# A hybrid encoder layer on one core: the products in the order v, k, q, the last gate's halves between them three, one, two, and the first weights on ScalarE's queue

## The chip, the cores and the metric

The kernel runs on one core of a Trainium2 chip. Its time is the device time of one execution in microseconds (us); less is better. The core's engines are named as the profile names them: PE (TensorE's matmuls; PEld its weight loads), DVE (VectorE), ACT (ScalarE), POOL (GpSimd) and SP (SyncE, which issues most of the DMAs). Each engine takes its instructions in the order in which the program lists them and waits, where it must, at the head of its own queue.

## The reference, cut to what matters

One layer on 512 tokens of width 1024. The normalised input is projected to 8192 columns: a pooling branch, an LRU branch, q, k and v of an attention with eight heads of 128, and three gates of 1024 columns each.

```python
h = rms_norm(x, norm_mix[l])
proj = jnp.einsum('bsd,dc->bsc', h, w_in[l])
u_pool, u_lru, q, k, v, g_logits = jnp.split(proj, splits, axis=-1)
gates = jax.nn.sigmoid(g_logits + b_gate[l]).reshape(B, S, N_BRANCH, D_MODEL)
...
qh = rms_norm(q.reshape(B, S, SB_HEADS, SB_HEAD_DIM), q_norm[l])
kh = rms_norm(k.reshape(B, S, SB_HEADS, SB_HEAD_DIM), k_norm[l])
vh = v.reshape(B, S, SB_HEADS, SB_HEAD_DIM)
y_sb = stick_breaking_attention(qh, kh, vh).reshape(B, S, SB_WIDTH)
merged = (gates[:, :, 0] * jnp.einsum('bsc,cd->bsd', y_pool, w_branch[l, 0])
          + gates[:, :, 1] * jnp.einsum('bsc,cd->bsd', y_lru, w_branch[l, 1])
          + gates[:, :, 2] * jnp.einsum('bsc,cd->bsd', y_sb, w_branch[l, 2]))
x = x + jnp.einsum('bsd,de->bse', merged, w_out[l])
```

A SwiGLU network with its own norm and residual follows. q and k are normed per head, v is not. The three products do not depend on each other; the attention needs all three.

## The kernel before

**Arithmetic.** Every weight is float32 and is used as a high and a low part: ACT copies the raw weights to `whi` (line 101), DVE subtracts that from the raw weights into `wlo` (line 102), and PE makes three matmuls of a pair (high by high, high by low, low by high). `raw`, `whi` and `wlo` have three buffers each, so the weights of a half can be made ready when the half three places ahead of it has been used.

**Stages.** (1) The head: token tiles `xt` and the first weights `raw0` are loaded, split (`hu`, `hi0`, `lo0`), and PE runs eight matmuls on a constant tile (`WARM`, line 349) until they are there; then come the gates of the first branch. (2) The LRU projections in four chunks with the second branch's gates between them; the LRU's own work (convolution, gates, scans) runs beside PE on ACT and DVE and reaches into stage 3. (3) q, k and v, described below. (4) The pooling branch, with the attention's work for eight heads spread over it and over the branch products of stage 5. (6) The output projection, (7) the network.

**The products q, k and v.** Each 1024 by 1024 product is done with seven block products instead of eight, named in `ORDER` (line 131): "11", "12", "S2", "S1", "S3", "S4", "22"; the S ones use sums of weight blocks, which DVE makes (`qkv_sum`, line 145). A block product has two halves of twelve matmuls (`tok_product`, lines 703 to 715, matmuls on line 712), each with its own pair `whi`, `wlo`. PE accumulates in PSUM; ACT copies a first part out (`snap`, line 722), DVE adds the rest (`final`, line 726). That leaves four blocks r of a product, (0,0), (1,1), (0,1) and (1,0), in this order. `post` (line 678) then norms q and k: ACT squares the block, DVE sums the squares (line 683) and scales the sum (line 684), POOL raises it to the power -1/2 (`rsqq`, line 256), and DVE refines this in four small instructions (lines 257 to 260). For q the result, `qrs`, goes with its negative (line 700) into the scale of a later sigmoid, so the block itself is stored as it is; for k, `krs`, ACT multiplies the block in eight instructions (line 698) before it is stored. The stores go out on POOL's queue into `qd`, from which the attention loads its heads (`at`, line 889).

**The third branch's gates.** Four chunks of 256 columns, each in two halves of 24 matmuls (`half_chunk`). The last chunk runs in stage 4; the six halves of the others stand between the block products, at the places in `AFTER` (line 172): after "12", "S3" and "22" of q and of k. The third product, v, has none.

**What sets the order.** The program is recorded in the order of the code; small tasks stand in lists (`bg`, `abg`) from which `tick` takes one after each piece of PE work. A scheduler then orders each engine's instructions by priorities, which `tc.high_priority` raises for weight splits. The order is fixed when the kernel is built.

Of the kernel before, what the change touches and what calls it, by code (L numbers as in the profile page):

```python
# [25 lines left out]
QSCALE = float(HD) ** -0.5  # L26
NEG = -1.0e30
EARLY = 300
WARM = 8
GBUFS = 27  # L30
NDIRECT = 2
KD = 4
# [31 lines left out]
def layer_kernel(ctx: ExitStack, tc: tile.TileContext, x, xt, vecs, w_in, w_pool, w_rg, w_ig,  # L64
                 w_branch, w_out, w_fg, w_fu, w_fd, out):
    nc = tc.nc
# [14 lines left out]
    def b4(shape, name, tag="b", dt=F32):  # L81
        bufs = {"w": NAW, "t": NAT, "b": NAB}[tag]
        return pools["ap0"].tile([P] + shape, dt, tag=tag, name=name, bufs=bufs)
# [5 lines left out]
    def cols(ap, k0, nk, c0, nc_):  # L89
        return ap[k0 * P:(k0 + nk) * P, c0:c0 + nc_].rearrange("(k p) c -> p k c", p=P)  # L90
# [25 lines left out]
    def add_gate(br, c):  # L116
        add_chunk256(("gate", br, c), w_in, 5120 + br * 1024 + c * 256)
# [14 lines left out]
    WITH = {"11": "11", "12": "21", "S2": "T2", "S1": "T1", "S3": "T3", "S4": "22", "22": "T4"}  # L132
    CH = {"11": 0, "12": 0, "21": 1, "22": 1}
    KH = {"11": 0, "12": 1, "21": 0, "22": 1}
    qraw = {}

    def qkv_raw(t, nm, i):
        if (t, nm, i) not in qraw:
            qraw[t, nm, i] = r = b4([2, 512], f"qw{t}{nm}{i}", "w")
            nc.sync.dma_start(r, cols(w_in, 4 * KH[nm] + 2 * i, 2, 2048 + t * 1024 + CH[nm] * 512, 512))  # L140
        return qraw[t, nm, i]
# [27 lines left out]


    AFTER = {}
    for n, (t, nm) in enumerate(((0, "12"), (0, "S3"), (0, "22"), (1, "12"), (1, "S3"), (1, "22"))):
        AFTER[t, nm] = divmod(n, 2)

    for n in range(4):
        add_direct(("first", n), cols(w_in, 2 * n, 2, 5120, 512), 2, 512)
# [2 lines left out]
    for n in (0, 1, 2, 4, 3, 5, 6, 7):  # L179
        if n < 4:  # L180
            add_lru(n)
        else:
            add_gate(1, n - 4)
    for t in range(3):
        for nm in ORDER:
            add_seven(t, nm, 0)
            add_seven(t, nm, 1)
            if (t, nm) in AFTER:
                c, half = AFTER[t, nm]
                add_direct(("gate", 2, c, half), cols(w_in, 4 * half, 4, 7168 + c * 256, 256), 4, 256)  # L190
# [41 lines left out]
    vt = cst.tile([P, NV], F32, tag="vt", name="vt")  # L232
# [102 lines left out]
    with ExitStack() as first:  # L335
# [11 lines left out]
        wps = pb.tile([P, 2, S], F32, tag="mm", name="warm_ps")  # L347
        for i in range(WARM):
            nc.tensor.matmul(wps[:, 0, :], warm[:, 0:P], warm, start=True, stop=True)
# [21 lines left out]
        raw0 = wp.tile([P, 2, 512], F32, tag="raw", name="raw0")  # L371
        ready["first", 0] = hi0, lo0
        src0 = cols(w_in, 0, 2, 5120, 512)
        nc.scalar.dma_start(vt, vecs)
        for k in range(2):
            load_xt(k)
            nc.sync.dma_start(raw0[:, k, :], src0[:, k, :])
            dve.tensor_copy(hi0[:, k, :], raw0[:, k, :])
            dve.tensor_tensor(lo0[:, k, :], raw0[:, k, :], hi0[:, k, :].bitcast(F32), ALU.subtract)
            make_h(k)  # L380
# [293 lines left out]
        def store(t, i, j, r):  # L674
            nc.gpsimd.dma_start(rows(t, i, j), r)


        def post(t, i, j, r):
            if t < 2:
                sq = b4([2, 512], f"sq{t}{i}{j}")  # L680
                s_ = cst.tile([P, 8], F32, tag="ssq", name=f"ssq{t}{i}{j}", bufs=2)
                act(sq, r, AF.Square)
                dve.tensor_reduce(s_, sq.rearrange("p a (b d) -> p (a b) d", d=HD), AX.X, ALU.add)
                dve.tensor_scalar(s_, s_, 1.0 / HD, EPS, ALU.mult, ALU.add)
                bg.append(lambda: post2(t, i, j, r, s_))
            else:
                store(t, i, j, r)

        def post2(t, i, j, r, s_):

            y = cst.tile([P, 8], F32, tag="krs", name=f"krs{i}{j}", bufs=2) if t else \
                qrs[:, 0, 2 * j:2 * j + 2, 4 * i:4 * i + 4]
            y3 = y.rearrange("p (a b) -> p a b", a=2) if t else y
            rsqrt(y3, s_.rearrange("p (a b) -> p a b", a=2), (2, 4), f"q{t}{i}{j}")
            if t:
                v = r.rearrange("p a (b d) -> p (a b) d", d=HD)
                for n in range(8):
                    act(v[:, n, :], v[:, n, :], AF.Copy, scale=y[:, n:n + 1])
            else:
                dve.tensor_scalar(qrs[:, 1, 2 * j:2 * j + 2, 4 * i:4 * i + 4], y3, -1.0, None, ALU.mult)  # L700
            store(t, i, j, r)

        def tok_product(t, nm, ps, first):
            bh, bl = BQ[WITH[nm]]
# [10 lines left out]
                    tick()  # L715

        gate2 = {}
        for t in range(3):
            ps = {}
            r = {}  # L720

            def snap(key, src):
                r[key] = b4([2, 512], f"r{t}{key[0]}{key[1]}")
                act(r[key], src, AF.Copy)

            def final(key, src):
                dve.tensor_tensor(r[key], r[key], src, ALU.add)
                bg.append(lambda t=t, key=key, v=r[key]: post(t, *key, v))

            def bank(nm):  # L730
                ps[nm] = pb.tile([P, 2, 512], F32, tag="mm", name=f"ps_q{t}{nm}")
                return ps[nm]

            for nm in ORDER:
                if nm in ("11", "12", "S1", "22"):
                    bank(nm)
                dst = {"S2": "11", "S3": "11", "S4": "S1"}.get(nm, nm)
                tok_product(t, nm, ps[dst], dst == nm)
                if nm == "11":
                    snap((0, 0), ps["11"])  # L740
                elif nm == "12":
                    final((0, 0), ps["12"])
                elif nm == "S2":
                    snap((0, 1), ps["11"])
                elif nm == "S1":
                    snap((1, 1), ps["S1"])
                elif nm == "S3":
                    final((1, 1), ps["11"])
                    snap((1, 0), ps["11"])
                elif nm == "S4":  # L750
                    final((0, 1), ps["S1"])
                else:
                    final((1, 0), ps["22"])
                if (t, nm) == (0, "S3"):
                    for f, c in ((lru_input, 3), (lru_scan, 2), (lru_scan, 3), (lru_store, 2), (lru_store, 3)):
                        step(of(f, c))
                if (t, nm) in AFTER:
                    c, half = AFTER[t, nm]
                    if half == 0:
                        gate2[c] = chunk_psum(("gate", 2, c), pb)  # L760
                    half_chunk(gate2[c], ("gate", 2, c), half, hn, 1)
                    if half == 1:
                        gate_store(2, c, gate2[c], True)
# [258 lines left out]
    with ExitStack() as ffn:  # L1022
# [21 lines left out]
        for c in range(4):  # L1044
# [5 lines left out]
            for j in range(2):  # L1050
                k = 2 * c + j
                if c % 2 == 0:
                    x1p[c // 2, j] = mp.tile([P, 2, S], F32, tag="m", name=f"x1{c}{j}")
                t = x1p[c // 2, j][:, c % 2, :]
# [77 lines left out]
        CH = {"11": 0, "12": 0, "21": 1, "22": 1}  # L1132
        KH = {"11": 0, "12": 1, "21": 0, "22": 1}

# [6 lines left out]
        def load_a(c):  # L1141
            for nm in ("11", "21", "22", "12"):
                raw[c, nm] = t = corner([2, 4, P], f"w{c}_{nm}")
                for w in range(2):
                    if c < DOWN:
                        ap, c0 = (w_fg, w_fu)[w], c * 256
                    else:
                        ap, c0 = w_fd, (c - DOWN) * 512 + w * 256
                    nc.sync.dma_start(t[:, w], cols(ap, KH[nm] * 4, 4, c0 + CH[nm] * P, P))

# [100 lines left out]
        for m in range(4):  # L1251
            t = fp.tile([P, 2, S], F32, tag="mm", name=f"ps_d{m}")
# [38 lines left out]
        for kc in range(KD, last + 1):  # L1291
            split_act(kc + 1)
            ah, al = split.pop(kc)
            for e in range(2):
# [3 lines left out]
                for j in range(4):  # L1298
# [5 lines left out]
                    if kc == last:  # L1304
                        t = x1[m]
# [64 lines left out]
```

## Time and profile before

| what | value |
|---|---|
| median of 3 runs | 939.15 us (937.56 to 939.16) |
| the profiled execution | 938.85 us, span 937.0 us |
| mean granted TensorE clock over the span | 0.998 |
| PE, DVE, ACT, POOL busy, share of the span | 99%, 76%, 52%, 5% |
| DMA | 124.13 MB, mean 132 GB/s |
| first product q, k, v (us from the span's start) | about 144 to 300 |

The span is the time from the first to the last instruction of the profiled execution; its own time is 1.85 us more. In a row of the timeline the first number is the start, the second the time busy, then engine, line, operation, output and inputs; in square brackets stands how long the engine had been idle and what ended that. A row of waits has the total, the number of waits and the longest. The starts of matmuls are the thing to read: their ends overlap.

### The profile page before, as it was taken

Reading aid. Unit: us, or ns where it says so; the run is one execution under the profiler, and the core shown is the slowest. Engines: PE = TensorE matmul, PEld = TensorE weight load, DVE = VectorE, ACT = ScalarE, POOL = GpSimd, SP = SyncE. Lnnn points to the kernel's source line nnn. Section 1 sums busy time; section 2 is a strip of 40 time slices with the busy share of each in tenths; the row PEclk is TensorE's granted clock in tenths of the full one; section 3 lists DMA queues with packets and bytes.
Section 4 is the critical chain, followed back from the end, with each engine's and each line's share of the span. In section 5 each row is a group of like instructions: output and inputs, shape, how many; then the busy total and the mean of one; then the engine's idle time right before and its main releaser. Section 6 shows DMA issues by size and latency. Waiting matters only on the chain.

```text
span 937.0 us, 13039 instructions
## 1 busy us (share of the span) xinstructions
PE 925.5 (99%) x5090; PEld 796.5 (85%) x5090; DVE 709.8 (76%) x890; ACT 489.6 (52%) x660; POOL 45.2 (5%) x69
## 2 busy tenths in 40 slices
PE   9999999899999999999999999999999999999998
PEld 6888778787878888788888888889999999988898
DVE  6797889777696699866865545699888888787465
ACT  6545997545655465644643234454554555653232
POOL 2000000222121000000000000000000000000000
PEclk9999999999999999999999999999999999999999
DMA  9484351652714934155532344355533334523001
GB/s 333 124 286 135 113 180 68 211 171 68 247 58 145 281 117 130 61 166 173 153 91 90 98 136 149 91 143 141 144 91 97 106 105 138 165 97 105 1 29 63
DMA packets 126894, 124.13 MB, mean 132 GB/s; under 512 B 7408, under 2 KB 105712, under 8 KB 126832
## 3 DMA queue, kind: packets, MB, share of 16 engines
q1 hardware_dynamic: 122800, 109.07, 38.2%
q0 software_dynamic: 3888, 14.16, 4.4%
q8 instruction: 40, 0.66, 0.3%
q14 instruction: 22, 0.18, 0.1%
q10 hardware_dynamic: 144, 0.06, 0.0%
HBM read 107.02 MB, written 16.25 MB: 132 GB/s over the span
## 4 chain that ended last, share of the span: by engine, by line
PE 82%; DVE 8%; ACT 5%; issue 3%; POOL 2%; DMA 0%; POOLq 0%; DVEq 0%; ACTq 0%
PE ps_y L1182 11%; PE ps_x L1182 8%; PE ps_br L227 5%; PE ps_br L229 5%; PE ps_br L228 5%; PE ps_q L712 3%; PE ps_d L227 3%; PE ps_d L228 3%; PE ps_d L229 3%; PE ps_gate L625 3%; PE ps_dy L1182 2%; DVE wlo L102 2%; PE ps_gate L227 2%; PE ps_gate L228 2%; PE ps_gate L229 2%
## 5 line engine op out<-in xcount | busy, mean ns | idle before, releaser
L101 ACT ACTIVATE whi<-raw 128x1024 fp32r<-128x1024 f32 x93 | 98.4, 1058 | 149.1 <-PE ps_br L228 46.2
L102 DVE TENSOR_TENSOR wlo<-raw,whi 128x1024 fp32r<-128x1024 f32 x93 | 113.5, 1221 | 63.8 <-ACT whi L101 58.6
L1172 ACT ACTIVATE wh_S<-w_S 128x1024 fp32r<-128x1024 f32 x44 | 46.6, 1061 | 56.6 <-PE ps_y L1182 25.6
L1173 DVE TENSOR_TENSOR wl_S<-w_S,wh_S 128x1024 fp32r<-128x1024 f32 x44 | 53.6, 1221 | 12.8 <-ACT wh_S L1172 12.6
L1172 ACT ACTIVATE wh<-w 128x1024 fp32r<-128x1024 f32 x33 | 35.0, 1062 | 49.0 <-issue 12.9
L102 DVE TENSOR_TENSOR wlo<-qw,whi 128x1024 fp32r<-128x1024 f32 x36 | 43.9, 1220 | 17.3 <-ACT whi L101 17.2
L1173 DVE TENSOR_TENSOR wl<-w,wh 128x1024 fp32r<-128x1024 f32 x33 | 40.3, 1222 | 17.4 <-ACT wh L1172 17.4
L101 ACT ACTIVATE whi<-qw 128x1024 fp32r<-128x1024 f32 x36 | 37.9, 1055 | 26.1 <-PE ps_q L712 17.6
L227 PE MATMUL ps_gate<-HH,whi 128*128 128x512 f32 x128 | 50.1, 392 | 0.0
L229 PE MATMUL ps_gate<-HH,wlo 128*128 128x512 f32 x128 | 49.9, 390 | 0.0
L228 PE MATMUL ps_gate<-HL,whi 128*128 128x512 f32 x128 | 49.8, 389 | 0.0
L227 PE MATMUL ps_d<-ah,whi 128*128 128x512 f32 x112 | 43.7, 391 | 0.0
L228 PE MATMUL ps_d<-al,whi 128*128 128x512 f32 x112 | 43.6, 389 | 0.0
L229 PE MATMUL ps_d<-ah,wlo 128*128 128x512 f32 x112 | 43.6, 389 | 0.0
L1160 DVE TENSOR_TENSOR w_S<-w,w 128x1024 f32<-128x1024 f32 x22 | 26.9, 1223 | 3.4 <-PE ps_d L228 2.9
L229 PEld LDWEIGHTS ps_gate<-HH,wlo 128*128 128x128 f32 x128 | 24.0, 188 | 5.3 <-DVE wlo L102 0.4
L227 PEld LDWEIGHTS ps_gate<-HH,whi 128*128 128x128 f32 x128 | 24.0, 188 | 5.2 <-issue 0.4
L228 PEld LDWEIGHTS ps_gate<-HL,whi 128*128 128x128 f32 x128 | 24.0, 188 | 4.9
L1160 DVE TENSOR_TENSOR w_S<-w,w_S 128x1024 f32<-128x1024 f32 x22 | 26.9, 1223 | 0.6
L933 DVE TENSOR_TENSOR_SCAN E<-K,zero 128x511 f32<-128x511 f32 (+3 forms) x32 | 25.5, 812 | 1.1 <-ACT K L928 1.1
L227 PE MATMUL ps_br<-yph,whi 128*128 128x512 f32 x64 | 25.6, 400 | 0.0
L227 PE MATMUL ps_pool<-HH,whi 128*128 128x512 f32 x64 | 25.6, 400 | 0.0
(634 smaller groups left out, 3015.7 us busy)
## 6 DMA issues: line engine op xcount, KB each, us to landing
raw<-in_w_in_dram SPq DMA_DIRECT2D x39, 512.0 KB, 4.9
qw<-in_w_in_dram SPq DMA_DIRECT2D x24, 512.0 KB, 4.7
raw<-in_w_branch_dram SPq DMA_DIRECT2D x24, 512.0 KB, 3.5
w<-in_w_ffn_gate_dram SPq DMA_DIRECT2D x36, 256.0 KB, 3.8
w<-in_w_ffn_up_dram SPq DMA_DIRECT2D x36, 256.0 KB, 4.2
raw<-in_w_ffn_down_dram SPq DMA_DIRECT2D x14, 512.0 KB, 3.5
qd<-r POOLq DMA_DIRECT2D x12, 512.0 KB, 3.4
at<-qd SPq DMA_DIRECT2D x24, 256.0 KB, 5.5
```

What stands on the lines that cost most here:

```text
L101: act(hi, raw, AF.Copy)
L102: dve.tensor_tensor(lo, raw, hi.bitcast(F32), ALU.subtract)
L227: nc.tensor.matmul(ps, lh, rh, start=start, stop=False, skip_group_check=skip)
L228: nc.tensor.matmul(ps, lh, rl, start=False, stop=False, skip_group_check=skip)
L229: nc.tensor.matmul(ps, ll, rh, start=False, stop=stop, skip_group_check=skip)
L625: nc.tensor.matmul(pss[n // 2][n % 2], w[:, k % 2, n * P:(n + 1) * P], hu[k][x_], start=k == 0 and w is wh and x_ == 0, stop=k == KT - 1 a ...
L712: nc.tensor.matmul(ps[:, a, :], b_[:, k, ts_], a_[:, kk, :], start=first and n == k == 0, stop=n == 2 and k == 3, skip_group_check=True)
L933: dve.tensor_tensor_scan(E[:, f - 1:c0 + n - 1][:, ::-1], K[:, f:c0 + n][:, ::-1], zero[:, 0:1].to_broadcast([P, c0 + n - f]), 1.0, ALU.mu ...
L1160: dve.tensor_tensor(t, raw[c, x], raw[c, y], op)
L1172: act(h, raw[c, nm], AF.Copy)
L1173: dve.tensor_tensor(l, raw[c, nm], h.bitcast(F32), ALU.subtract)
L1182: nc.tensor.matmul(o, a[:, w, k, :], b[:, k, :], start=first and n == k == 0, stop=n == 2 and k == 3, skip_group_check=True)
```

## The change

Four edits. The three products run in the order v, k, q instead of q, k, v (`VKQ`), weights and products alike. The six halves of the third branch's gates stand three in the first product (after "12", "S3", "22"), one in the second (after "12") and two in the third (after "11" and "S2"). A block of q is stored straight from `post`, as v's is, instead of after its norm; k's is stored after the norm as before. In the head, the small vectors `vt` are loaded first on SP's queue, and the first half of the first weights is loaded first on ACT's queue; there are seven warm-up matmuls instead of eight.

```diff
-WARM = 8
+WARM = 7
...
+    VKQ = (2, 1, 0)
...
-    for n, (t, nm) in enumerate(((0, "12"), (0, "S3"), (0, "22"), (1, "12"), (1, "S3"), (1, "22"))):
-        AFTER[t, nm] = divmod(n, 2)
+    for n, (t, nm) in enumerate(((0, "12"), (0, "S3"), (0, "22"), (1, "12"), (2, "11"), (2, "S2"))):
+        AFTER[VKQ[t], nm] = divmod(n, 2)
...
-    for t in range(3):
+    for t in VKQ:
         for nm in ORDER:
             add_seven(t, nm, 0)
             add_seven(t, nm, 1)
...
-        nc.scalar.dma_start(vt, vecs)
+        nc.sync.dma_start(vt, vecs)
         for k in range(2):
             load_xt(k)
-            nc.sync.dma_start(raw0[:, k, :], src0[:, k, :])
+            (nc.sync if k else nc.scalar).dma_start(raw0[:, k, :], src0[:, k, :])
...
                 bg.append(lambda: post2(t, i, j, r, s_))
-            else:
+            if t != 1:
                 store(t, i, j, r)
...
                     act(v[:, n, :], v[:, n, :], AF.Copy, scale=y[:, n:n + 1])
+                store(t, i, j, r)
             else:
                 dve.tensor_scalar(qrs[:, 1, 2 * j:2 * j + 2, 4 * i:4 * i + 4], y3, -1.0, None, ALU.mult)
-            store(t, i, j, r)
...
-        for t in range(3):
+        for t in VKQ:
             ps = {}
...
-                if (t, nm) == (0, "S3"):
+                if (t, nm) == (VKQ[0], "S3"):
                     for f, c in ((lru_input, 3), (lru_scan, 2), (lru_scan, 3), (lru_store, 2), (lru_store, 3)):
```

**How the order moves.** The lines of the changed kernel are one higher from line 135 on. Rows name the engine's instructions; a number behind an underscore tells one buffer from another.

DVE in the first product, around the block products S1 and S3, before (the two `wlo` from `qw_1250` and `qw_1322` are S1's halves, the one from `qw_1208` is the first half of S3; `ls`, `li`, `lt` are the LRU's):

```order
L727 TENSOR_TENSOR r_1348<-r_1348,ps_q_1350 128x1024
L603 SCALAR_TENSOR_TENSOR ls_1201<-lr_1060,ls_1201 128x1024
L610 SCALAR_TENSOR_TENSOR li_882<-lt_1096,ls_1199 128x512
L683 TENSOR_REDUCE ssq_1415<-sq_1414 128x8
L102 TENSOR_TENSOR wlo_1441<-qw_1250,whi_1440 128x1024
L684 TENSOR_SCALAR ssq_1415<-ssq_1415 128x8
L604 TENSOR_TENSOR ls_1201<-ls_1201,li_1061 128x1024
L102 TENSOR_TENSOR wlo_1458<-qw_1322,whi_1457 128x1024
L257 TENSOR_TENSOR qrs<-rsqq_1431 128x2x4
L610 SCALAR_TENSOR_TENSOR li_882<-lt_1096,ls_1199 128x512
```

Behind them stand two more scans (L610) with two of q's small instructions between them, and then S3's first `wlo`, from `qw_1208`. In the change (S1's halves from `qw_1249` and `qw_1321`, S3's first from `qw_1207`):

```order
L728 TENSOR_TENSOR r_1347<-r_1347,ps_q_1349 128x1024
L604 SCALAR_TENSOR_TENSOR ls_1200<-lr_1059,ls_1200 128x1024
L611 SCALAR_TENSOR_TENSOR li_881<-lt_1095,ls_1198 128x512
L605 TENSOR_TENSOR ls_1200<-ls_1200,li_1060 128x1024
L102 TENSOR_TENSOR wlo_1428<-qw_1249,whi_1427 128x1024
L611 SCALAR_TENSOR_TENSOR li_881<-lt_1095,ls_1198 128x512
L611 SCALAR_TENSOR_TENSOR li_1060<-lt_1178,ls_1200 128x512
L102 TENSOR_TENSOR wlo_1445<-qw_1321,whi_1444 128x1024
L611 SCALAR_TENSOR_TENSOR li_1060<-lt_1178,ls_1200 128x512
L102 TENSOR_TENSOR wlo_1464<-qw_1207,whi_1463 128x1024
```

The sum of squares and the small instructions on `qrs` are gone from here, the LRU's rows stay; two scans now stand ahead of S1's second `wlo`, one ahead of S3's first.

ACT in the second product, k, from the square of its first block on, before (`whi_1873` and `whi_1890` are S1's halves):

```order
L682 ACTIVATE sq_1835<-r_1777 128x1024
L101 ACTIVATE whi_1873<-qw_1693 128x1024
L698 ACTIVATE r_1777<-r_1777,krs_1852 128x128 x7
L101 ACTIVATE whi_1890<-qw_1758 128x1024
L698 ACTIVATE r_1777<-r_1777,krs_1852 128x128
L502 ACTIVATE gt_1868<-ps_gate_1_1686,vt 128x512 x2
```

and in the change (`whi_1824` and `whi_1841`), behind the square of the same block:

```order
L699 ACTIVATE r_1728<-r_1728,krs_1803 128x128 x3
L101 ACTIVATE whi_1824<-qw_1656 128x1024
L699 ACTIVATE r_1728<-r_1728,krs_1803 128x128 x5
L503 ACTIVATE gt_1819<-ps_gate_1_1649,vt 128x512
L101 ACTIVATE whi_1841<-qw_1709 128x1024
L503 ACTIVATE gt_1819<-ps_gate_1_1649,vt 128x512
```

Three of the eight multiplications by k's norm, which wait for DVE and POOL, now stand ahead of S1's first high half, and one sigmoid of the gate ahead of its second.

SP's first DMAs, before (`vt` is on ACT's queue then):

```order
L358 DMA xt_131<-in_xt_dram 128x512
L377 DMA raw_137<-in_w_in_dram 128x512
L358 DMA xt_131<-in_xt_dram 128x512
L377 DMA raw_137<-in_w_in_dram 128x512
L358 DMA xt_132<-in_xt_dram 128x512
```

and in the change, where ACT's queue begins with the other half of `raw_136`:

```order
L375 DMA vt<-in_vecs_dram 128x114
L359 DMA xt_130<-in_xt_dram 128x512 x2
L378 DMA raw_136<-in_w_in_dram 128x512
L359 DMA xt_131<-in_xt_dram 128x512
L108 DMA raw_153<-in_w_in_dram 128x2x512
```

The first tokens move from the first to the second place on SP, the first weights from SP's second place to ACT's first, and the second tokens stay ahead of the second weights.

## The prediction

> **What bounds the kernel now.** I read the page's shares first, then who TensorE waited for, then the rows around its longest wait.
>
> ```profile
> span 937.0 us, 13039 instructions
> PE 925.5 (99%) x5090; PEld 796.5 (85%) x5090; DVE 709.8 (76%) x890; ACT 489.6 (52%) x660; POOL 45.2 (5%) x69
> ```
>
> The profiled execution took 938.85 us, 1.85 us more than its span; it lies 0.30 us under the median of the runs, 939.15. TensorE (PE) is busy 99% of the span, so only what makes it wait or run slowly can be won. Its waits, longest first, up to 300 us and behind that:
>
> ```profile
> PE ps_q L712 <- DVE wlo L102: 2.5, 1, 2.5
> PE ps_gate L625 <- DVE whi L378: 0.9, 1, 0.9
> PE ps_q1S L712 <- DVE wlo L102: 0.8, 2, 0.5
> PE pw L947 <- DVE ypl L842: 0.9, 1, 0.9
> ```
>
> Three of the four lie in what the change touches: the first product of the three, the head, and the second product. The longest, in order of time:
>
> ```profile
> 171.24 0.39 PE L712 MATMUL ps_q0S<-whi,hT1h 128*128 128x512 f32 x1
> 173.96 0.39 PE L712 MATMUL ps_q<-whi,hT3h 128*128 128x512 f32 x1
> 176.89 0.79 PE L712 MATMUL ps_q<-wlo,hT3h 128*128 128x512 f32 x1 [2.55 <-DVE wlo L102]
> 177.49 0.63 PE L712 MATMUL ps_q<-whi,hT3l 128*128 128x512 f32 x1
> 180.41 0.40 PE L712 MATMUL ps_q<-whi,hT3h 128*128 128x512 f32 x1
> ```
>
> The twelve matmuls of one half of a product, 171.24 to 173.96, take 2.72 us, 0.227 from one to the next. Behind the wait the seven from 177.49 to 180.41 start 0.42 apart, then 0.227 again: PE was at half its rate. From 173.96 to 180.41 nine matmuls started in 6.45 us, where 9 x 0.227 = 2.04 would do: **the stall costs 4.41 us**, 2.70 of them the wait and 1.71 the slow stretch behind it. The rows of VectorE (DVE), ACT and POOL say why the low half was late:
>
> ```profile
> 163.54 1.22 DVE L603 SCALAR_TENSOR_TENSOR ls<-lr,ls 128x1024 f32<-128x1024 f32 x1
> 164.68 1.22 DVE L610 TENSOR_TENSOR_SCAN li<-lt,ls 128x512 f32<-128x512 f32 x1
> 168.31 3.69 POOL L256 TENSOR_TENSOR rsqq<-ssq,mhalf 128x8 f32<-128x8 f32 x1 [3.66 <-DVE ssq L684]
> 168.78 1.06 ACT L101 ACTIVATE whi<-qw 128x1024 fp32r<-128x1024 f32 x1 [1.66 <-PE ps_q L712]
> 169.26 1.22 DVE L102 TENSOR_TENSOR wlo<-qw,whi 128x1024 fp32r<-128x1024 f32 x1
> 172.04 0.17 DVE L257 TENSOR_TENSOR qrs<-rsqq 128x8 f32<-128x8 f32 x1 [1.56 <-POOL rsqq L256]
> 172.12 1.22 DVE L610 TENSOR_TENSOR_SCAN li<-lt,ls 128x512 f32<-128x512 f32 x1
> 173.31 1.22 DVE L610 TENSOR_TENSOR_SCAN li<-lt,ls 128x512 f32<-128x512 f32 x1
> 175.64 1.20 DVE L102 TENSOR_TENSOR wlo<-qw,whi 128x1024 fp32r<-128x1024 f32 x1
> ```
>
> The high half that PE wanted was ready at 169.84, but its low half stood in DVE's queue behind the first instruction of the norm (L257), and that waited for POOL's power of 3.69 us. Three scans of the LRU branch, queued behind it, came next. The norm of q, in the product that shares DVE with the end of the LRU work, is what makes this place late.
>
> **The first product becomes v.** It has no norm: the sum of squares, POOL's power and the seven small instructions of each block leave this place, the LRU rows stay. I lay the new order on the old rows, 1.14 us from one large instruction to the next (163.54 to 164.68) and 1.19 behind a scan (172.12 to 173.31). Scan 164.68; product of LRU input 165.87; low half of S1's first half 167.01; two scans 168.15 and 169.34; low half of S1's second half 170.53 to 171.75; the last scan 171.67; low half of S3 172.86 to 174.08. PE wants S1's second low half at 171.24 + 0.23 = 171.47 and so waits 0.3 us; S3's it wants at 174.26 + 0.23 = 174.49, and has it. So the term is -4.41 + 0.3 = **-4.1 us**. For the wait that stays, the bounds are 0 (two scans placed 0.3 us better) and 1.0, about the longest wait that the trace has without a slow stretch behind it: after 0.9 at L947 and the two of 0.5 and 0.3 below, matmuls go on at full rate.
>
> **The second product.** It stays k, with its norm, but without q's norms in front of it. Now:
>
> ```profile
> 220.59 0.17 DVE L257 TENSOR_TENSOR qrs<-rsqq 128x8 f32<-128x8 f32 x1 [1.47 <-POOL rsqq L256]
> 220.67 1.22 DVE L727 TENSOR_TENSOR r<-r,ps_q 128x1024 f32<-128x1024 f32 x1
> 227.34 0.39 PE L712 MATMUL ps_q1S<-whi,hT1h 128*128 128x512 f32 x1
> 228.22 0.50 PE L712 MATMUL ps_q1S<-wlo,hT1h 128*128 128x512 f32 x1 [0.50 <-DVE wlo L102]
> 230.85 0.39 PE L712 MATMUL ps_q1S<-whi,hT1h 128*128 128x512 f32 x1
> 231.55 0.50 PE L712 MATMUL ps_q1S<-wlo,hT1h 128*128 128x512 f32 x1 [0.31 <-DVE wlo L102]
> L256 POOL TENSOR_TENSOR rsqq<-ssq,mhalf x8: 1636/2496/3695, 168.3 to 273.3; 128x8 f32<-128x8 f32 x8
> 227.13 2.16 ACT L698 ACTIVATE r<-r,krs 128x128 f32<-128x128 f32 x7 [3.19 <-DVE krs L260]
> ```
>
> Two late low halves: 0.88 - 0.23 = 0.65 and 0.70 - 0.23 = 0.47 us, and the two matmuls behind the waits take 0.50 instead of 0.39: 1.3 us together. PE's product "12" is done 48 matmuls (gate half and S2, 10.9 us) ahead of 227.34, at 216.5, yet DVE adds it up only at 220.67, behind q's norm. Without that norm: sum 216.7, low half 217.9, reduce 219.1, its scaling done 220.5, POOL's power (1.64 where DVE waits for it) 220.6 to 222.3, four small ones to 223.1. ACT's new order puts three scalings ahead of S1's high half: 224.1 to 225.2, low half to 226.4, wanted at 227.57: 1.1 us early. Five more scalings (1.6) and a sigmoid (0.6) go ahead of the next: low half to 229.4, wanted at 230.29. The wait goes: -1.3; with POOL at its longest, 3.70, it is 2.06 later, and 1.0 of wait comes back: -0.3. I take **-1.2**.
>
> **The gate halves.** k loses two of its three, PE rows of 24 x 0.227 = 5.44 us each that ask of DVE one low half alone. From k's S1 to q's first gate half nothing gives DVE air. There DVE has 16 large instructions in the new order, 16 x 1.14 = 18.2 us, and PE ten halves of 2.72 = 27.2: enough. From there to q's second gate half it has 14, 16.0 us, and 1.0 of small ones against 5.44 + 4 x 2.72 = 16.3 us of PE: 0.7 too much, within the 1.9 us by which the last of these low halves is early (it may start once the half three places ahead is used, 5.4 us before it is wanted, and needs 2.4 for its two instructions). q's norms then wait for POOL under the second gate half, whose 5.44 us of PE need only one low half. Price **0**, bounds 0 and +0.7 (one POOL turn of 3.70 less 3.0 of cover). All gate work, LRU work and stores are the same in number; v's stores go out early, q's at once without its norm.
>
> **The head,** as it is now:
>
> ```profile
> 1.19 0.44 SPq L377 DMA_DIRECT2D raw<-in_w_in_dram  x1
> DMA to landing us min/median/max: 3.2/4.3/5.3
> 1.46 3.60 PE L349 MATMUL warm_ps<-warm 128*128 128x512 bf16 x8 [1.46 <-DVE warm L241]
> 3.92 0.72 ACT L364 ACTIVATE hu<-xt,vt 128x512 fp32r<-128x512 f32 x1 [1.16 <-DMA xt<-in_xt_dram]
> 4.68 0.75 DVE L365 SCALAR_TENSOR_TENSOR hu<-xt,vt,hu 128x512 fp32r<-128x512 f32 x1 [0.40 <-ACT hu L364]
> 5.35 0.42 DVE L378 CAST whi<-raw 128x512 fp32r<-128x512 f32 x1
> 5.91 2.05 PE L625 MATMUL ps_gate<-hu,whi 128*128 128x512 f32 x4 [0.86 <-DVE whi L378]
> 9.46 0.72 PE L625 MATMUL ps_gate<-hu,whi 128*128 128x512 f32 x2
> ```
>
> The answer on L377 has the shortest landing, 3.2, for the first of its two loads: the first weights, second on SP's queue, are there at 1.19 + 3.2 = 4.4. DVE's cast of them comes at 5.35 only, since the low half of the tokens stands ahead of it, and PE starts 0.14 behind the cast (5.77 to 5.91). In the change the weights go out first and the cast is early; the first tokens take the weights' place, second on SP behind the vectors, with the same bytes ahead of them. If they land at 4.4 as the weights do now, 4.4 + 0.1 + 0.72 of ACT + 0.14 gives a start at 5.4, 0.5 earlier. The eight matmuls up to 9.46 run at half rate (3.60 / 8 = 0.45 each in the warm-up); if full rate comes at the same time as now, 0.5 / 0.45 = 1.1 more matmuls fit in before it, 0.25 us. I take **-0.4**; bounds 0 (tokens later still) and -0.5. The warm-up matmul that goes, 0.45 us, ends before either start.
>
> **The sum:** -4.1 - 1.2 + 0 - 0.4 = -5.7; 938.85 - 5.7 = **933.1 us**, 0.6% less.
>
> **The rivals.** *The stall moves into the second product*: the same miss as now, with its slow stretch, where the gate halves went. For it speaks that DVE has no air there, against it the sums above. Price +4.41: 937.5, no change that can be told. Chance 0.10.
>
> *Part of the first stall stays*: DVE's rows above leave no gap but the one for POOL, so one other row late by 0.7 us makes the wait 1.0 and the slow stretch of 1.71 may come again: 933.1 + 0.7 + 1.7 = 935.5. Chance 0.13.
>
> *Full rate comes earlier in the head*: the slow stretch behind the stall lasted 3.5 us (176.89 to 180.41). Were the gap ahead of the first product short enough not to count, full rate would come such a stretch sooner, 8 matmuls at 0.2 less: 933.1 - 1.6 = 931.5. The gap hardly shrinks (4.6 to 5.4 against 5.05 to 5.91). Chance 0.12. [...]
>
> *Slower: the attention's first loads come late.* q is last now, so its norms fall into the start of the pool stage.
>
> ```profile
> 302.82 1.23 DVE L102 TENSOR_TENSOR wlo<-raw,whi 128x1024 fp32r<-128x1024 f32 x1 [1.37 <-ACT whi L101]
> 304.61 1.48 SPq L889 DMA_DIRECT2D at<-qd  x3
> 310.91 0.82 PE L896 MATMUL pq<-idn,at 128*128 128x128 f32 x6
> at<-qd SPq DMA_DIRECT2D x24, 256.0 KB, 5.5
> ```
>
> The loads of the first head stand in SP's queue behind a weight load that waits for the low half at 302.82; 304.61 + 5.5 = 310.1, 0.8 us ahead of the transposes. In the new order two first instructions of q's norm, each with a POOL turn, stand ahead of that low half. If both came with 3.70 at the wrong time, the loads would be 7.4 late, PE would wait 6.6 and run slowly for 1.7: 933.1 + 8.3 = 941.4. It is slower than before from 4.8 us of lateness on (0.8 + 5.7 - 1.7). Against it: both POOL turns begin with blocks that are done 5 us and more before the product ends, so they should be over by then. Chance 0.05.
>
> **How the numbers follow.** The forecast has 0.60. Terms at their good ends give 938.85 - 4.4 - 1.3 - 0.5 - 1.6 = 931.0, at their bad ends 938.85 - 3.4 - 0.3 + 0.7 = 935.8; I set **930.9 to 936.6**, which leaves out the first and the last rival. Under 0.2% of 939 (1.9 us) a measurement can't tell from no change. Faster: 0.60 + 0.13 + 0.12 and a little of the first rival, 0.87; same 0.08; slower 0.05.
>
> **What would show it.** No wait over 0.5 us at L712 in the first product, and no matmuls 0.42 us apart behind the first 10 us; no L256 on POOL before the second product; no wait at 228; first product matmul at 5.4. It would be wrong if L712 waits over 1 us anywhere, if PE waits for the transposes at L896, or if the head starts later than 5.9.

## The result, and the profile after

The changed kernel took 932.80 us in the median of four executions (930.87 to 933.13), against 938.44 us before (937.56 to 939.16, four executions on the same chips): the ratio is 0.9936, with a 95% interval from 0.9918 to 0.9954. The forecast was 933.1 us. The profiled execution after the change took 930.87 us with a span of 928.7; the one before had taken 938.85 with a span of 937.0. That difference, 7.98 us, is more than the one between the medians, and a part of this section goes to why.

The page's shares after the change, and then the answer on who PE waited for (engine, line, what it waited for; us in total, times, longest):

```profile
span 928.7 us, 13041 instructions
PE 920.8 (99%) x5089; PEld 794.2 (86%) x5089; DVE 709.6 (76%) x890; ACT 490.6 (53%) x660; POOL 38.3 (4%) x69
```

```profile
PE warm_ps L350 <- DVE warm L242: 1.5, 1, 1.5
PE pw L948 <- DVE ypl L843: 0.9, 1, 0.9
PE ps_gate L626 <- ACT hu L365: 0.7, 1, 0.7
PE pps L228 <- ACT ysb L964: 0.5, 1, 0.5
PE pq L897 <- PE pq L897: 0.3, 1, 0.3
```

Both waits at the line of the products (now L713) are gone. DVE does the same work as before (709.6 us against 709.8); POOL is busy 6.9 us less, and not because it does less:

```profile
L257 POOL TENSOR_TENSOR rsqq<-ssq,mhalf x8: 1637/1659/1665, 214.2 to 298.0; 128x8 f32<-128x8 f32 x8
```

The eight powers of the norms, which had taken 1.64 to 3.70 us, take 1.64 to 1.67 each, and the first stands at 214, in the second product. In the first product PE now runs through, but for one hesitation (rows of PE and of DVE, in order of time):

```profile
168.13 1.20 DVE L102 TENSOR_TENSOR wlo<-qw,whi 128x1024 fp32r<-128x1024 f32 x1
169.02 0.39 PE L713 MATMUL ps_q2S<-whi,hT1h 128*128 128x512 f32 x1
169.38 0.50 PE L713 MATMUL ps_q2S<-wlo,hT1h 128*128 128x512 f32 x1
169.72 0.39 PE L713 MATMUL ps_q2S<-whi,hT1l 128*128 128x512 f32 x1
172.01 0.39 PE L713 MATMUL ps_q<-whi,hT3h 128*128 128x512 f32 x1
172.24 0.39 PE L713 MATMUL ps_q<-wlo,hT3h 128*128 128x512 f32 x1
```

The second low half of S1 ends at 169.33; the matmul on it starts at 169.38 instead of 169.25, and the next 0.34 later instead of 0.227: 0.25 us in all. At S3, where 2.55 us had been waited, the two matmuls are 0.23 apart. The head, and there the difference between this execution and the one shown of before:

```profile
1.46 3.17 PE L350 MATMUL warm_ps<-warm 128*128 128x512 bf16 x7 [1.46 <-DVE warm L242]
5.37 1.19 PE L626 MATMUL ps_gate<-hu,whi 128*128 128x512 f32 x4 [0.74 <-ACT hu L365]
6.40 1.08 PE L626 MATMUL ps_gate<-hu,wlo 128*128 128x512 f32 x4
7.32 1.98 PE L626 MATMUL ps_gate<-hu,whi 128*128 128x512 f32 x8
```

The first product matmul starts at 5.37 (before: 5.91), and the first eight take 1.95 us (5.37 to 7.32), where they had taken 3.55 (5.91 to 9.46): PE has its full rate from the first one on. Stretch by stretch, from the starts of the matmuls, what they lose against 0.227 from one to the next:

| stretch | before | after | difference | forecast |
|---|---|---|---|---|
| head: start of the first product matmul | 5.91 | 5.37 | -0.54 | -0.5, of it -0.4 to the end |
| head: the first eight matmuls | 3.55 | 1.95 | -1.60 | 0 (a rival: -1.6) |
| first product | 4.41 | 0.25 | -4.16 | -4.1 |
| second product | 1.35 | 0 | -1.35 | -1.2 |
| third product | 0.49 | 0 | -0.49 | 0 |

They sum to -8.14; the spans differ by 8.3.

The -1.60 is not the change's alone. The times of both kernels fall into two groups with nothing between them. Over all 47 executions of the kernel before that the runs below were measured against, 19 lie between 936.89 and 937.46 us and 28 between 938.51 and 939.70 (the four of the result beside them: 937.56, 937.73, 939.15 and 939.16); of 14 executions of the change (two runs below repeat it) five lie between 930.63 and 931.03, and nine between 932.50 and 933.45. In the 14 traces of this case the execution was in the lower group where full rate was there at the start of the first product, or came 0.7 us behind it (run d1 below), and in the upper where it came 3.5 us or more behind it. (Four kernels below have only one group; by this mark each goes with one of the change's.) Group against group, the change gains 6.5 and 6.3 us on one chip (medians 937.20 to 930.74 and 938.98 to 932.70) and 6.5 and 6.0 on another (937.20 to 930.68, 938.86 to 932.85), about what the other four rows say (-6.5). The group is named below as lower or upper.

### The profile page after: what moved, and what is told of

It reads as the page before. It is cut to its first block, busy times and chain, and to the rows that moved or that the text cites. A ratio compares the mean times of both kernels' runs of the same rounds, so it can differ in the third digit from the quotient of the medians.

```text
span 928.7 us, 13041 instructions
## 1 busy us (share of the span) xinstructions
PE 920.8 (99%) x5089; PEld 794.2 (86%) x5089; DVE 709.6 (76%) x890; ACT 490.6 (53%) x660; POOL 38.3 (4%) x69
## 4 chain that ended last, share of the span: by engine, by line
PE 98%; DVE 1%; DMA 0%; issue 0%; ACT 0%; SPq 0%; DVEq 0%; ACTq 0%
PE ps_y L1183 11%; PE ps_q L713 9%; PE ps_x L1183 8%; PE ps_br L228 5%; PE ps_br L230 5%; PE ps_br L229 5%; PE ps_gate L230 4%; PE ps_gate L228 4%; PE ps_gate L229 4%; PE ps_d L228 3%; PE ps_d L229 3%; PE ps_d L230 3%; PE ps_dy L1183 2%; PE ps_gate L626 2%; PE ps_dx L1183 2%; PE ps_lru L228 2%
## 5 line engine op out<-in xcount | busy, mean ns | idle before, releaser
L102 DVE TENSOR_TENSOR wlo<-raw,whi 128x1024 fp32r<-128x1024 f32 x93 | 113.6, 1222 | 55.1 <-ACT whi L101 53.9
L102 DVE TENSOR_TENSOR wlo<-qw,whi 128x1024 fp32r<-128x1024 f32 x36 | 43.9, 1221 | 23.5 <-ACT whi L101 23.5
```

The costliest lines, as they stand in the source:

```text
L102: dve.tensor_tensor(lo, raw, hi.bitcast(F32), ALU.subtract)
```

## The experiments

### The change taken apart

Four kernels, on one chip. Run a1 has the order alone (with the store of q's blocks that it needs):

```diff
+    VKQ = (2, 1, 0)
...
-        AFTER[t, nm] = divmod(n, 2)
+        AFTER[VKQ[t], nm] = divmod(n, 2)
...
-    for t in range(3):
+    for t in VKQ:
...
```

> Only the order v, k, q (with the plain store of q's blocks); the third gate's halves stand three, three, none by place, the head as before. If the order alone carries the gain: no wait of TensorE at the line of the products in the first one, no slow stretch there, -4.4 us; the second product without its two waits, -1.3; about 933 us. If the gate halves in the third product are needed, q's own norms and k's last ones meet a third product without gate work, and a wait of 1 to 3 us with or without a slow stretch of 1.7 shows there: 935 to 938 us.

Run a2 has in addition the gate halves as in the change, three, one, two; it lacks only the head.

> The whole change without its head (eight warm-up matmuls, the queues of the first loads as before). If the head is worth what its earlier start shows (0.5 us), 933.2 us, that is 938.85 - 4.4 - 1.3, and the first product matmul at 5.9 at half rate until about 9.6. If the moved gate halves do anything, it is the difference to the run with the order alone.

Run a3 has the head alone (`WARM = 7`, the queues of the first loads), run a4 the gate halves alone:

```diff
-    ... (0, "22"), (1, "12"), (1, "S3"), (1, "22"))):
+    ... (0, "22"), (1, "12"), (2, "11"), (2, "S2"))):
```

> Only the head: seven warm-up matmuls, first weights on ScalarE's queue, vectors on SP. The stalls in the products stay as they are (4.4 and 1.3 us). First product matmul at 5.4 instead of 5.9, so 938.3 us if the matmuls behind it run at half rate until 9 to 10 us as before; if full rate comes with the warm-up, 8 matmuls at 0.2 us less, about 936.6. If the point at which full rate comes is a matter of phase, single executions show both, some 1.7 us apart.

> Only the gate halves moved (three, one, two), products still q, k, v, head as before. The stall of 4.4 us in q stays. If the halves are worth nothing by themselves: 939 us. If they were the air that the second product lived on: its waits grow from 1.3 to 2 to 6 us, and the time is 940 to 944 us.

| kernel | lower group | upper group | median of all | ratio to before |
|---|---|---|---|---|
| before (23 executions) | 936.89 to 937.46 | 938.51 to 939.65 | 938.56 | |
| a1, order | 933.39 to 933.64 | 935.39, 935.75 | 933.64 | 0.9959 (0.9946 to 0.9972) |
| a2, order and gate halves | 931.15 | 932.91 to 933.21 | 933.08 | 0.9942 (0.9930 to 0.9954) |
| a3, head | 936.62 to 936.85 | 938.53 to 939.16 | 938.71 | 0.9997 (0.9987 to 1.0006) |
| a4, gate halves | 936.38 to 937.11 | 938.36 to 938.85 | 938.42 | 0.9997 (0.9989 to 1.0006) |

The order alone is worth 3.5 to 3.7 us, group against group, and not the 5.7 that the first case expected: its third product waits, as the second case has it, though three of its five executions lie below the 935 to 938 us of that case. PE and DVE there, in a1:

```profile
276.47 0.42 PE L713 MATMUL ps_q<-whi,hT3h 128*128 128x512 f32 x1
277.85 0.50 PE L713 MATMUL ps_q<-wlo,hT3h 128*128 128x512 f32 x1 [0.95 <-DVE wlo L102]
```

```profile
273.73 0.17 DVE L685 TENSOR_SCALAR ssq<-ssq 128x8 f32<-128x8 f32 x1
275.74 0.17 DVE L258 TENSOR_TENSOR qrs<-rsqq 128x8 f32<-128x8 f32 x1 [1.85 <-POOL rsqq L257]
276.57 1.22 DVE L102 TENSOR_TENSOR wlo<-qw,whi 128x1024 fp32r<-128x1024 f32 x1
```

It is the old pattern in the new place: a low half stands behind the first small instruction of q's norm, which waits 1.85 us for POOL. With a start that is 0.25 late at 268.28 and the late matmuls behind both, the third product of a1 loses 1.69 us. Run a2, with two gate halves in that product, has no entry for the line of the products among its waits. So the halves are worth 1.7 us there, once the order is v, k, q; the 0.6 us that remain of the 2.3 to 2.4 between a1 and a2 are a wait of the pooling stage at 297.28 on DVE's addition (L728), which comes back further down.

The halves alone leave the stall and the second product's waits exactly as they were:

```profile
PE ps_q L712 <- DVE wlo L102: 2.5, 1, 2.5
PE ps_q1S L712 <- DVE wlo L102: 0.8, 2, 0.5
```

So the first of the two cases expected of a4 came, nearly: it is 0.4 to 0.5 us faster in the medians of the groups, since a late half of 0.49 us in the third product of before is gone, and the median of all executions doesn't show it. The second product, which has two halves less, waits no more than before.

The head alone starts at 5.48 (rows of a3; a4, with the old head, at 5.94), and is worth 0.3 us in the lower group and 0.1 in the upper. Its executions fall into two groups 2.2 us apart, as the case of the phase has it (it expected 1.7).

```profile
1.46 3.17 PE L349 MATMUL warm_ps<-warm 128*128 128x512 bf16 x7 [1.46 <-DVE warm L241]
5.48 2.07 PE L625 MATMUL ps_gate<-hu,whi 128*128 128x512 f32 x4 [0.85 <-ACT hu L364]
```

### Is it the norm, and is it POOL's turn in it?

Run b1 is the change in which v gets a norm too; its result goes nowhere.

```diff
-            if t < 2:
+            if t < 3:
                 sq = b4([2, 512], f"sq{t}{i}{j}")
...
-            if t:
+            if t == 2:
+                dve.tensor_scalar(y3, y3, -1.0, None, ALU.mult)
+            elif t:
```

> The change with a norm computed for v too (sum of squares, POOL's power, the small instructions; its result is used nowhere). If the norm in the first place was the cause of the stall: the low half of S3 stands again behind POOL's power, a wait of about 2.5 us and a slow stretch of 1.7 come back in the first product, and the second product waits about 1.3 again: +5 to +6 us on the change, 936 to 938.5 us. If the stall hung on something else of q (its weights, its place in the buffers): within 0.5 us of the change.

It took 935.90 to 936.80 in six executions and 937.64 to 938.61 in five (median 936.80, ratio to before 0.9987, 0.9979 to 0.9996; the change beside it 930.68, and 932.50 to 933.45): 4.9 to 5.3 us more than the change, group against group, at the lower end of what was expected. The stall is there again, to the tenth:

```profile
165.95 3.69 POOL L257 TENSOR_TENSOR rsqq<-ssq,mhalf 128x8 f32<-128x8 f32 x1 [3.66 <-DVE ssq L685]
```

```profile
169.68 0.17 DVE L258 TENSOR_TENSOR krs<-rsqq 128x8 f32<-128x8 f32 x1 [1.55 <-POOL rsqq L257]
173.28 1.20 DVE L102 TENSOR_TENSOR wlo<-qw,whi 128x1024 fp32r<-128x1024 f32 x1
```

```profile
PE ps_q L715 <- DVE wlo L102: 2.5, 1, 2.5
PE ps_q1S L715 <- DVE wlo L102: 0.8, 2, 0.5
```

The stall doesn't hang on q, its weights or its buffers: a norm of v in that place makes it as well, and the next product's two late low halves come along.

Run b2 is the kernel before in which q's norms lose only POOL's power; a copy of 8 columns on DVE stands in its place.

```diff
+        if pool:
             nc.gpsimd.tensor_tensor(t, ms, e, ALU.pow)
+        else:
+            dve.tensor_copy(t, ms)
...
-            rsqrt(y3, ..., f"q{t}{i}{j}")
+            rsqrt(y3, ..., f"q{t}{i}{j}", t > 0)
```

> The kernel before, in which q's norms leave out POOL's power: a copy of 8 columns on VectorE stands in its place, all other instructions of the norm stay (so q's norm is not the reference's). If POOL's turn made the low half late: VectorE goes on 1.5 us earlier there, the wait of 2.5 becomes about 1.1 with or without a slow stretch behind it, and the second product's waits of 1.3 shrink: 2.5 to 4.6 us less than before, 933 to 936.5 us. If the number of instructions on VectorE made it late: less than 1 us faster.

It took 932.05, and 934.07 to 934.37 in four executions (before: 937.16 to 937.31, and 938.56 to 939.29; ratio 0.9956, 0.9943 to 0.9968): 4.6 to 5.2 us less, group against group, a little beyond the 4.6 expected at most.

```profile
170.49 0.17 DVE L259 COPY rsqq<-ssq 128x8 f32<-128x8 f32 x1
174.07 1.20 DVE L102 TENSOR_TENSOR wlo<-qw,whi 128x1024 fp32r<-128x1024 f32 x1
```

```profile
174.07 0.39 PE L715 MATMUL ps_q<-whi,hT3h 128*128 128x512 f32 x1
175.33 0.50 PE L715 MATMUL ps_q<-wlo,hT3h 128*128 128x512 f32 x1 [0.88 <-DVE wlo L102]
175.67 0.40 PE L715 MATMUL ps_q<-whi,hT3l 128*128 128x512 f32 x1
```

DVE goes on at 170.49 instead of standing still until 172.04, S3's low half starts 1.57 us earlier (174.07 against 175.64), and the wait is 0.88 instead of 2.55. No slow stretch follows: the next matmul comes 0.34 later, the one after it 0.24. The second product doesn't wait at all. So the 1.6 us by which POOL held DVE made most of the stall of 4.41: the run loses 1.15 us in this place, that is 1.67 less of wait and no slow stretch. The 1.15 (0.88, and the late matmuls on either side) is DVE's own work.

### What decides at which rate the first product runs

The change itself, and the same with eight, nine and five warm-up matmuls. The windows in the expectations are steps of 3.41 us; what the traces show of them, half rate for 3.413 us behind each long stall and PE busy for 75% or more of the 3.413 us ahead of full rate, is in the last section.

> The change itself once more, as the measure for the three runs beside it: 931 or 932.8 us by execution. Theory: full rate comes at the end of one of a series of windows of 3.41 us whose phase differs from run to run, if TensorE was busy for about three quarters of it. With seven warm-up matmuls it is busy from 1.46 to 4.42 or 4.85, and again from 5.37: some 2 in 5 executions get full rate by 5.3 us (930.9), the others at 8.7 to 10.8 (932.5 to 933.3).

> The change with eight warm-up matmuls instead of seven; they end at 4.85 or 5.3, still ahead of the first product at 5.37. Theory of the windows: every window from the warm-up on is now at least 85% busy, full rate comes at 4.0 to 7.4 us in every execution, so all lie between 930.8 and 931.9 us, and none at 932.5 or more. Rival, the warm-up doesn't decide: 931 and 932.8 mixed as with seven.

> The change with nine warm-up matmuls, which end at 5.30, 0.07 us ahead of the first product at half rate. Theory of the windows: as with eight, 930.8 to 931.9 us in all executions. If the warm-up runs into the first product, its start moves behind 5.4 and the time is up to 0.4 us longer.

> The change with five warm-up matmuls, over by 3.6 to 4.0 us. Theory of the windows: no window ahead of the first product is three quarters busy, so no execution has full rate early: all at 932.3 to 933.6 us, none at 931. Rival, the warm-up doesn't decide: 931 and 932.8 mixed as with seven.

The first rows of PE in these four, in the same order:

```profile
1.46 3.17 PE L350 MATMUL warm_ps<-warm 128*128 128x512 bf16 x7 [1.46 <-DVE warm L242]
5.32 2.07 PE L626 MATMUL ps_gate<-hu,whi 128*128 128x512 f32 x4 [0.70 <-ACT hu L365]
```

```profile
1.46 3.22 PE L350 MATMUL warm_ps<-warm 128*128 128x512 bf16 x8 [1.46 <-DVE warm L242]
5.32 1.19 PE L626 MATMUL ps_gate<-hu,whi 128*128 128x512 f32 x4 [0.64 <-ACT hu L365]
```

```profile
1.46 3.96 PE L350 MATMUL warm_ps<-warm 128*128 128x512 bf16 x9 [1.46 <-DVE warm L242]
5.29 1.20 PE L626 MATMUL ps_gate<-hu,whi 128*128 128x512 f32 x4
```

```profile
1.46 2.31 PE L350 MATMUL warm_ps<-warm 128*128 128x512 bf16 x5 [1.46 <-DVE warm L242]
5.28 2.08 PE L626 MATMUL ps_gate<-hu,whi 128*128 128x512 f32 x4 [1.51 <-ACT hu L365]
```

| warm-up | executions, us | ratio to before |
|---|---|---|
| 5 of 512 | 932.29, 932.73, 932.87, 932.96, 933.18 | 0.9941 (0.9928 to 0.9953) |
| 7 of 512 (the change) | 930.63, 930.74, 931.03, 932.60, 932.80 | 0.9927 (0.9914 to 0.9941) |
| 8 of 512 | 931.34, 931.47, 931.58, 931.63, 932.12 | 0.9928 (0.9916 to 0.9940) |
| 9 of 512 | 931.27, 931.41, 931.46, 931.47, 931.86 | 0.9927 (0.9914 to 0.9941) |

With five, all are in the upper group; with eight or nine, none; with seven, both occur. The theory holds in this, and its rival falls. One execution with eight, 932.12, is above the 931.9 expected. But eight and nine are 0.7 to 0.8 us above the lower group of seven, and 0.6 of that is a wait which the change doesn't have (a row of the run with eight; nine has it at the same place):

```profile
294.79 0.50 PE L228 MATMUL ps_pool<-HH,whi 128*128 128x512 f32 x1 [0.32 <-DVE r L728]
```

The engines' orders are the same with seven and eight, apart from the warm-up. What differs is the semaphore on which the first matmul of the second pooling block waits in the trace: PE's with five and seven, DVE's with eight and nine. My reading is that the PSUM buffer of the block is chosen when the kernel is built, and that another warm-up can give it one that DVE's addition of the last product's part (L728) holds for longer; the traces don't number the buffers, so this is argued and not shown. Nor is it the length of the warm-up alone: with eight and the old head, a2 waits on PE there and a1 on DVE. Nine warm-up matmuls of 448 columns keep PE busy nearly as long as eight of 512 (3.54 us in run d1, 3.60 in before), and with them the matmul waits on PE:

```diff
-        for i in range(WARM):
-            nc.tensor.matmul(wps[:, 0, :], warm[:, 0:P], warm, start=True, stop=True)
+        for i in range(9):
+            nc.tensor.matmul(wps[:, 0, 0:448], warm[:, 0:P], warm[:, 0:448], start=True, stop=True)
```

> The change with nine warm-up matmuls of 448 columns instead of seven of 512: at half rate they end at about 4.8 us as eight of 512 do, and the PSUM buffer of the second pooling block is the one that the change itself has there, with no addition of VectorE in front of it. Theory of the windows: all executions early, and without the 0.48 us at 294 us that eight and nine of 512 columns showed: 930.6 to 931.7 us, median about 930.9. If that wait was not a matter of the buffer: 931.3 to 932.1 as with eight.

> The change itself on this chip, as the measure for the runs beside it: a mix of about 930.9 and 932.8 us.

It took 930.99, 931.12, 931.27, 931.62 and 931.64 us; the change beside it 930.68, 932.50, 932.61, 933.08 and 933.45. All five are in the lower group, and the wait at the pooling block is gone from the trace.

```profile
1.46 3.54 PE L350 MATMUL warm_ps<-warm 128*128 128x448 bf16 x9 [1.46 <-DVE warm L242]
5.42 1.49 PE L626 MATMUL ps_gate<-hu,whi 128*128 128x512 f32 x4 [0.42 <-ACT hu L365]
```

The median expected, 930.9, was too low: in the profiled execution full rate came inside the first four matmuls (1.49 us, neither 1.19 nor 2.07). Its ratio to before is 0.9929 (0.9916 to 0.9943), that of the change on this chip 0.9941 (0.9929 to 0.9954). The intervals overlap, so a faster median is not shown. What is shown is that none of five executions lost the 1.9 us that four of the change's five lost.

## Why the prediction was right, point by point

**The first product: right, in place and size.** -4.1 was forecast, -4.16 measured. The wait of 0.3 us that the laid-out rows left at S1's second low half is there, with 0.25, and it is at that matmul. Run b1 shows the norm as the cause, run b2 POOL's turn as the larger part of it: the reading "its low half stood in DVE's queue behind L257" was the right one. (The working counts seven small instructions of a block; beside the sum of squares there are six, which changes no term.)

**The second product: right.** -1.2 of 1.3 was taken, 1.35 went. The reason given, that k waited because q's last norm stood ahead of its own, is borne out by b2 (k unchanged and in its old place, q's norm without POOL: no wait) and by b1 (v's norm ahead of k's: both waits back).

**The gate halves: the size was right, the reasoning too small.** The step priced them at 0, by showing that DVE has enough time without them in the second product. That holds (a4: the second product doesn't get worse). What the step called cover, "5.44 us of PE need only one low half", had no price of its own, and it should have had one: without the two halves in the third product the order loses 1.7 us there (a1 against a2). Alone, the order is worth 3.5 to 3.7 us and the halves 0.4 to 0.5; together they are worth 5.9 (a2), 1.8 to 2.0 more than the sum, of which 0.6 is the wait at 297.28.

**The third product: the term that was missing.** The trace of before has a late low half at 275 that I did not read, because it was not among the listed waits:

```profile
275.02 0.39 PE L712 MATMUL ps_q<-whi,hT2h 128*128 128x512 f32 x1
275.52 0.50 PE L712 MATMUL ps_q<-wlo,hT2h 128*128 128x512 f32 x1
```

The two are 0.50 apart instead of 0.227. With the late matmuls behind it this cost 0.49 us, and the change takes it away. The sum of the forecast, -5.7, with this term is -6.2; group against group -6.0 to -6.5 was measured.

**The head: right in the start, wrong in what a single execution means.** 5.4 was forecast for the start, 5.28 to 5.42 came in the eight traces with this head and the change's order. 0.4 was forecast as its worth; 0.1 to 0.3 was measured alone (a3), and a2 against the change gives 0.3 to 0.5 (on other chips), so the term is of the right size and not resolved more closely. The 0.45 us that the step takes for a warm-up matmul is too long, since it includes the tail of the last one: they start 0.427 apart in the trace of before, and the term hardly moves by it. The rival *full rate comes earlier* (931.5, chance 0.12) describes the profiled execution, but its reason, a shorter gap that no longer counts, is not what happens: by their times both kernels have both cases, the one before full rate early in 19 of 47 executions, the change in 5 of 14. The two times shown of before, 937.56 and 939.15, fit these two cases, and I had read them as noise. The sentence that set the rival aside, "the gap hardly shrinks", looked for a change where the executions of one kernel differ among themselves. It is luck, then, that 933.1 lies so near the median of 932.80: the profile from which the sum starts is in the upper group, and so are three of the four executions behind that median; from the lower group of before, 937.2, the same terms end at 931.5.

**The other rivals.** The stall did not move into the second product, and no part of it with a slow stretch stayed in the first. The attention's first loads did come nearer to being late:

```profile
297.01 1.75 SPq L890 DMA_DIRECT2D at<-qd  x3
302.58 1.03 PE L897 MATMUL pq<-idn,at 128*128 128x128 f32 x8
at<-qd SPq DMA_DIRECT2D x24, 256.0 KB, 5.1
```

Issue and median landing give 302.1, half a microsecond ahead of the transposes at 302.58 (before: 0.8). The reason given against this rival held for one of the two turns of POOL that stand ahead of the loads: the first began at 286.87 and was over when the product's last matmul started at 291.5, the second began at 291.86 only. Both took 1.66 us and not 3.70, so they did no harm.

## What to carry to other kernels

A stall that several things make together is best read from the row that stands still: DVE did nothing for 1.56 us with a ready instruction behind the one that waited, and removing that wait removes all of the stall but 0.25 us (another product first) or but 1.15 us (no POOL in the norm). An edit that shows nothing alone, as the gate halves here, may hold up the gain of another, so a change is taken apart in both directions. And where the times of one kernel fall into two groups, the cause is looked for first and the comparison is made group against group: here it was worth a third of the effect under study.

## What the runs showed of the hardware

**The points at which the rate changed lay whole steps of 3.413 us apart.** The traces record the stretches in which TensorE's granted clock was at full (1.0) and at half (0.5). In the four traces with the long stall (us from the span's start):

| trace | full rate from | half rate from, behind the stall | difference | in steps of 3.4133 |
|---|---|---|---|---|
| before | 9.639 | 176.892 | 167.253 | 49.0 |
| a3 | 10.531 | 177.784 | 167.253 | 49.0 |
| a4 | 10.050 | 177.303 | 167.253 | 49.0 |
| b1 | 5.104 | 175.770 | 170.666 | 50.0 |

The half-rate stretch lasts 3.413 us in each. In all 14 traces full rate ends behind the last matmul of the kernel, again a whole number of such steps after it began (221.0 or 222.0 behind the stall, 270.0 or 271.0 where there was none; in before it is 757.759 us and 222.0 steps, in the change 925.012 and 271.0). Counted back from there in these steps, the first such point lies 0.3 to 3.2 us after the start of the span, at another place in each of the four traces above (2.81, 0.29, 3.22 and 1.69).

How busy PE was in a step differs between those ahead of full rate and the others. With a half-rate matmul counted as 0.427 us from its start (the distance of the warm-up's starts in before), the step ahead of full rate was 75% to 100% busy in all 14 traces (75% in a1: warm-up from 2.29 to 4.85 of the 3.41 us up to 5.70). Of the earlier steps, with half rate behind them, the fullest had 73% (the run c4: 2.34 to 4.42 and 5.35 to 5.75 of the 3.41 us up to 5.75). The shares hang on this way of counting: by the modelled ends of the matmuls the two kinds overlap. In steps at full rate with waits in them, 66% (a1 at 276.5), 70% (b2) and 56% (two waits of the pooling stage in one step, before up to 388.5 and after up to 380.1) had full rate behind them; the 21% to 36% of the four long stalls had half rate for one step. An estimate from these counts, with 75% ahead of full rate and the point anywhere in a step: seven warm-up matmuls with a start at 5.35 give full rate early when the point lies between 4.02 and 5.28, in 1.26 / 3.41 = 37% of executions; it was 5 of 14. For the eight of before, with a start at 5.9, it is 4.02 to 5.70, 49%; it was 19 of 47. Why the rate changes at these points and at these shares, the traces don't show.

**POOL's power beside DVE's operations on two tensors in SBUF.** Two of the powers of before, and what DVE did beside the second (beside the first it stood still):

```profile
188.79 1.66 POOL L256 TENSOR_TENSOR rsqq<-ssq,mhalf 128x8 f32<-128x8 f32 x1 [2.53 <-DVE ssq L684]
...
198.83 2.67 POOL L256 TENSOR_TENSOR rsqq<-ssq,mhalf 128x8 f32<-128x8 f32 x1 [1.69 <-DVE ssq L684]
```

```profile
198.76 1.22 DVE L102 TENSOR_TENSOR wlo<-qw,whi 128x1024 fp32r<-128x1024 f32 x1
```

The low half ends at 199.98, and the power 1.52 us behind it. In the kernel before five of the eight powers took 2.50 to 3.70; each of these started while DVE ran a large operation on two tensors in SBUF (L102, L150, L604), and all five ended 1.52 to 1.53 us after the end of such an operation, two of them after the second of two in a row. At 273.34 a second one, begun 0.07 us before the first had ended, had no part in it: the power ended at 275.84, 1.53 us behind the end of the first. So which of two in a row counts stays open. For the one in the stall that was the low half which ended at 170.48; the power was over at 172.00. In the change all eight start when DVE is idle, in an instruction of 8 columns, or in an addition that reads PSUM (L728), and they take 1.64 to 1.67 us. Over all 14 traces it is the same: 20 of 112 powers started under such an operation and took 2.49 to 3.70, the 92 others took 1.64 to 1.67, 40 of them started under an addition that reads PSUM. The most that came on top beside such an operation is 2.06 us on 1.64 (3.70, the power in the stall). What holds the power there, the traces don't show.
